# Float32r products whose moving operands are read in turn from two rows of a block

## The chip, the core and the metric

The kernel runs on one core of a Trainium2 chip. The metric is the time of one execution on the device in microseconds (us): 1568.5 us is the median of three runs of the kernel before the change (1567.9 to 1571.1). One further execution was profiled; its trace gives the start and the length of every instruction.

The engines have short names in the profile: PE is TensorE (its matmuls), PEld its weight loads, DVE is VectorE, ACT is ScalarE, POOL is GpSimd, SP is SyncE, which issues transfers here. A product `T.matmul(out, lhsT=..., rhs=...)` appears twice: as an LDWEIGHTS, which loads the stationary operand `lhsT` (128 rows by up to 128 columns), and as a MATMUL, which streams the moving operand `rhs` past it, column by column, and adds the result into a bank of PSUM.

## What is computed

Two layers of a decoder trunk on 512 positions of width 1024, in float32. Cut to what matters:

```python
for i in range(DEPTH):                                  # 2 layers
    z = rmsnorm(x, mix_pre_g[i]) @ w_in[i]              # 1024 -> 3206
    ...                                                 # gating, retention, forgetting attention on parts of z
    x = x + rmsnorm(concat([out_a, out_b, out_c]) @ w_o[i], mix_post_g[i])

    h = rmsnorm(x, ffn_pre_g[i])                        # 1024 -> 4096 -> 1024
    g, up = h @ w_gate[i], h @ w_up[i]
    x = x + rmsnorm((gelu(causal_conv3(g)) * up) @ w_down[i], ffn_post_g[i])

    gate = sigmoid(rmsnorm(x, ple_pre_g[i]) @ w_ple_gate[i])
    x = x + rmsnorm((p[i] @ w_ple_proj[i]) * gate, ple_post_g[i])
```

Nearly all the arithmetic is in the products with the weights.

## The kernel before, in words

**Products in three parts.** To keep float32 accuracy, a large product is made of three float32r products. `split` (ACT and DVE) writes an operand as a high and a low part, both float32r; `mm3` (line 908) issues high x high, high x low and low x high into the same bank. `down` (line 1277) writes the same three out by hand.

**Two kinds of product.** In the first, activations are stationary and weights move: 128 positions by up to 512 columns of weights (`tm_mm`, `tm_chunk_major`, `down`, `embed`). These make the gating and value projections, the output projection (`out_proj`), the down projection, the gate of the last sub-layer (`ple`) and the embedding product. Their moving operands are 512 columns wide, 384 and 390 for the two value projections, and 256 in the last chunk of the last layer. In the second kind, weights are stationary and activations move, so that the result comes out with features on the partitions: `fm_mm` (512 positions at a time) and `seven`.

**`seven` (line 860)** makes a pair of 128-feature blocks (gate and up, or two blocks of the mixers) for all 512 positions with seven products of half size in place of eight, by a scheme of sums and differences (Strassen's, in Winograd's form). Each of the seven products has four contraction blocks, three float32r products each, 256 positions wide. They go to three banks, `be`, `al` and `ga`; bank `be` accumulates over several of them and is copied out in between, so that the next product into `be` waits for the copy before it. ACT and DVE empty the banks into `gs` and `us` (256 columns at a time). It is called 78 times: 32 times per layer for gate and up, 7 times per layer in the mixers. The weights of a call come as one raw tile, whose sums are made by DVE and by adding transfers, and which are split before use (`seven_weights`, line 837).

**The feed-forward part.** `gate_up(b)` for 32 blocks `b` makes one call of `seven`, the convolution, gelu and product with `us`, and splits the result into `acts`. Between the sixth and the seventh product of the call, `pieces` puts the down products of four blocks earlier in, so that each block has 84 products of 256 columns and, from the fifth block on, 24 of 512.

**The order of the work** isn't the order of the program. All calls of engines are recorded by `Plan`; `Plan.issue` (line 252) simulates the five engines with a price for each instruction (`cost`, line 209), picks for each engine the next ready instruction, and then emits everything in the order so found. The price of a float32r product is 0.4427 ns per column. Dependencies come from the regions that instructions touch: `region` (line 149) turns an access pattern into runs of addresses. Large tiles lie in two pools, `X` and `W`, with a small pad between (line 60 and 540); the split weights of `seven` lie in `W`, all other float32r tiles in `X`, except `wu`, which lies in the small work pool.

**Weights in DRAM** are laid out by `packed` (line 503), in numpy on the host, before the launch.

Of the kernel before, what the change touches and what calls it, by code (L numbers as in the profile page):

```python
# [29 lines left out]
F32R = mybir.dt.float32r  # L30
# [3 lines left out]
ALU = mybir.AluOpType  # L34
AX = mybir.AxisListType

P = 128
# [13 lines left out]
class Plan:  # L51
# [96 lines left out]
    @staticmethod  # L148
    def region(ap):
        dims = [tuple(d) for d in ap.ap]  # L150
        step, parts = dims[0]
        p0, f0 = divmod(ap.offset, step) if step else (0, ap.offset)
        runs = [(f0, f0 + 1)]
        for st, n in reversed(dims[1:]):
            if st == 0 or n == 1:
                continue
            lo, hi = runs[0]
            if len(runs) == 1 and st <= hi - lo:
                runs = [(lo, hi + st * (n - 1))]
            else:  # L160
                runs = [(a + i * st, b + i * st) for i in range(n) for a, b in runs]
        return p0, p0 + parts, runs
# [46 lines left out]
    def cost(self, engine, method, outs, ins, args, kw):  # L209

        def size(ap):
            n = 1
            for d in ap.shape[1:]:
                n *= d
            return n

        if "dma" in method:
            return (820 if engine == "POOL" else 525) if outs[0].shape[0] > 2 else 700, 4.0 * size(outs[0]) * outs[0].shape[0]
        n = size(ins[0] if method == "tensor_reduce" else outs[0])
        psum = any(self.tiles[v.tensor.name][3] for v in ins + outs)  # L220
        scalars = [kw.get(k) for k in ("scalar", "scalar1", "scalar2", "bias", "scale")]
        pointers = sum(isinstance(v, bass.AP) for v in scalars)
        if engine == "PE":
            if method == "transpose":
                return 108, 0, n, "T"
            dt, rows = kw["lhsT"].dtype, kw["lhsT"].shape[0] / P
            if dt in (F32R, BF16):
                return (0.4427 if dt == F32R else 0.42) * n, 0, n * rows, n
            if kw["lhsT"].shape[0] == 64 or kw["lhsT"].shape[-1] == 64:
                return 0.5 * (n * 4 / 2.4 + 4), 0, 2 * n * rows, "H"  # L230
            return max(222, n * 4 / 2.4 + 4), 0, 2 * n * rows, "F"
        if engine == "ACT":
            func = ([v for v in args if isinstance(v, AF)] + [None])[0]
            self.table[len(self.ops)] = func if func in self.TABLES else None
            pointers += method == "mul" and isinstance(args[2], bass.AP)
            if outs[0].shape[0] < 64:
                return 160 + n / 1.196, 0
            return (50 if psum else 97) + n / 1.196 + 93 * pointers + 93 * ("accum_out" in kw), 0
        if engine == "POOL":
            if n > 64:  # L240
                return 155 + n * (2.09 if method == "tensor_tensor" else 0.86), 0
            if kw.get("op") == ALU.pow:
                return 600 + 155 * n, 0
            return 420, 0
        rate = 0.96
        if method == "reciprocal":
            rate /= 8
        elif method in ("tensor_copy", "tensor_scalar") and not psum:
            rate *= 2
        return 68 + 62 * bool(pointers) + 68 * ("accum_out" in kw) + n / rate, 0  # L250
# [249 lines left out]
SEVEN = ("hb11", "hb21", "hh6", "hhd", "hh7", "hb22", "hh4")  # L500


def packed(w):

    def rows(m, order=None):

        m = m.reshape(-1, P, m.shape[-1])
        return (m if order is None else m[list(order)]).transpose(1, 0, 2)

    def blocks(m):  # L510

        return m.reshape(KB, P, -1, P).transpose(2, 1, 0, 3).reshape(-1, P, KB * P)

    r = {}
    r["uv"] = [rows(m[:, C_U:C_U + 512]) for m in w["w_in"]]
    r["rv"] = [rows(m[:, C_RV:C_RV + 384]) for m in w["w_in"]]
    r["fv"] = [rows(m[:, C_FV:C_FV + 390]) for m in w["w_in"]]
    def pairs(g, u):
        g, u = (blocks(m).reshape(-1, P, 2, 512) for m in (g, u))
        return np.stack([u[:, :, 1], u[:, :, 0], g[:, :, 0], g[:, :, 1]], 2)  # L520

    r["rg"] = [blocks(m[:, C_RG + 2 * P:C_RG + 3 * P])[0] for m in w["w_in"]]
    r["fm"] = [pairs(*(np.concatenate([m[:, p[i]:p[i] + P] for p in PAIRS], 1) for i in range(2))) for m in w["w_in"]]
    r["gu"] = [pairs(g, u) for g, u in zip(w["w_gate"], w["w_up"])]
    r["dn"] = [m.reshape(8, 4, P, 2, 512).transpose(0, 3, 2, 1, 4) for m in w["w_down"]]
    r["wo"] = [np.stack([rows(m[:, c:c + 512], O_ORDER) for c in (0, 512)]) for m in w["w_o"]]
    r["pg"] = [np.stack([rows(m[:, c:c + 512]) for c in (0, 512)]) for m in w["w_ple_gate"]]
    r["pe"] = [rows(m) for m in w["w_ple_proj"]]
    return {k: np.ascontiguousarray(np.stack(v)) for k, v in r.items()}


def body(ctx, tc, a, out):
    nc = tc.nc
    plan = Plan(tc)
    V, A, G, T, SY = (plan.engine(n, e) for n, e in (
        ("DVE", nc.vector), ("ACT", nc.scalar), ("POOL", nc.gpsimd), ("PE", nc.tensor), ("SP", nc.sync)))
# [130 lines left out]
    class Plain:  # L667
# [21 lines left out]
        def rhs(self, i, k):  # L689
            return self.t[i][k // 4][:, k % 4, :]  # L690

        def lhs(self, i, k, c):
            return self.t[i][k // 4][:, k % 4, c * P:c * P + P]
# [166 lines left out]
    def seven(h, ws, gs, us, scale=1.0, between=None):  # L860

        wg, wu, sa, sb = ws
        be, al, ga = (bank(n)[:, 0:256] for n in ("beta", "alpha", "gamma"))
        t1, t2 = slice(0, 256), slice(256, 512)

        def product(ps, w, n, first, last, part=range(4)):
            for k in part:
                ks = slice(k * P, k * P + P)
                mm3(ps, lambda i: w[i][:, ks], lambda i: h.part(n, i, k), first and k == 0, last and k == 3, True)

        def part(t, i):
            return [t[:, j, i * 512:i * 512 + 512] for j in range(2)]
        product(be, part(wg, 0), "b11", True, False)
        A.copy(gs[:, t1], be)
        product(al, part(wg, 1), "b21", True, True)
        V.tensor_tensor(out=gs[:, t1], in0=al, in1=gs[:, t1], op=ALU.add)
        product(be, part(sa, 0), "h6", False, False)
        A.copy(gs[:, t2], be)
        product(ga, part(sa, 1), "hd", True, False)
        if scale == 1.0:  # L880
            A.copy(us[:, t2], ga)
        else:
            A.mul(us[:, t2], ga, -scale)
        product(be, part(sb, 0), "h7", False, False)
        V.scalar_tensor_tensor(out=us[:, t2], in0=be, scalar=-scale, in1=us[:, t2], op0=ALU.mult, op1=ALU.subtract if scale == 1.0 else ALU.add)
        product(ga, part(sb, 1), "b22", False, True)
        V.tensor_tensor(out=gs[:, t2], in0=ga, in1=gs[:, t2], op=ALU.add)
        rest = between() if between else None
        product(be, wu, "h4", False, True, range(1) if rest else range(4))
        if rest:  # L890
            rest()
            product(be, wu, "h4", False, True, range(1, 4))
        A.mul(us[:, t1], be, -scale)

    def tm_units(src, n, nk=KB, parts=2, more=None):

# [8 lines left out]
                ts.append(t)  # L905
        return lambda i, k, c0=0, c1=n: ts[k // 2][:, i, k % 2, c0:c1]

    def mm3(ps, lhs, rhs, first, last, skip=False):
        for i, (h, r) in enumerate(((0, 0), (0, 1), (1, 0))):
            T.matmul(ps, lhsT=lhs(h), rhs=rhs(r), start=first and i == 0, stop=last and i == 2, skip_group_check=skip)  # L910

    def tm_mm(ps, act, k, c, u, first, last, c0=0, c1=512, j=None):
        mm3(ps, lambda i: act.lhs(i, k, c), lambda i: u(i, k if j is None else j, c0, c1), first, last)
# [27 lines left out]
    def mixers(l, hT, uv, ready):  # L941
# [162 lines left out]
        def ret_gate():  # L1104
            ps = bank("gps")
            fm_mm(ps, hT, fm_units(a["w_rg"][l]))
            A.copy(sg[:, 2, :], ps)

        def ret_proj(p):
            res = [wk("rm") for _ in range(2)]  # L1110
# [139 lines left out]
    def ffn(l, hs, emb, ready, x, new, g, nxt):  # L1250
# [3 lines left out]
        ps = bank("cpps")  # L1254
# [22 lines left out]
        def down(q, c, u, done):  # L1277

            ps = bank("dn")
            ts = slice(c * P, c * P + P)  # L1280
            for j in range(4):
                t = acts[2 * q + j // 2]
                for i, (h, r) in enumerate(((0, 0), (0, 1), (1, 0))):
                    if j < 3 or not i:
                        T.matmul(ps, lhsT=t[:, h, j % 2, ts], rhs=u(r, j), start=j == 0 and i == 0, stop=False)

            def rest():
                T.matmul(ps, lhsT=t[:, 0, 1, ts], rhs=u(1, 3), start=False, stop=False)
                T.matmul(ps, lhsT=t[:, 1, 1, ts], rhs=u(0, 3), start=False, stop=True)
                done(ps)  # L1290
            return rest

# [241 lines left out]
```

## Time and profile before

| | |
|---|---|
| median of three runs | 1568.5 us (1567.9 to 1571.1) |
| span of the profiled execution | 1564.8 us |
| PE busy | 1546.8 us, 99% |
| DVE busy | 1219.5 us, 78% |
| ACT busy | 888.6 us, 57% |
| granted TensorE clock | 0.998 |
| HBM traffic | 152 GB/s over the span |

The span runs from the first to the last instruction of the program; the runs are timed around the whole execution, so a median is a few us longer than a span. The profile gives no other time for its own execution.

How to read it: matmuls are pipelined, and the profile models their ends, so that one MATMUL's duration (some 280 ns for 256 columns) is longer than its share of the time. The pace of products is read from the distance between starts: the start of a run of products to the start of what follows, divided by their count. A group "A<-B,C 128x256 f32 x936 | busy, mean" says what is written, what is read, the shape, the count, the time in which at least one of them was under way, and the mean duration of one in ns. Idle time stands behind the second bar, with who ended it. All instructions are emitted by one line of the planner, L452, so groups are told apart by the names of their tiles: `dn` is the bank of the down product, `beta`, `alpha` and `gamma` those of `seven`, `ps` those of the other weight-moving products, `wo` the first half of the output projection, `eps` the embedding, `gps` one gate block.

### The profile page before, as it was taken

The numbers are of one execution on the slowest core, as the hardware profiler recorded it, in microseconds if no ns is written. First come the engines' busy times: TensorE is split into PE (matmuls) and PEld (weight loads), VectorE is DVE, ScalarE is ACT, GpSimd is POOL, SyncE is SP. The second block draws the span as 40 slices with busy tenths as digits, with TensorE's granted clock in tenths as the row PEclk, the third lists the DMA queues.
The fourth block names the chain that finished last, engine by engine and source line by source line (L and its number), as shares of the span: only waits on it lengthen the run. The fifth ranks groups of instructions, "written<-read, shape, count | busy, mean of one in ns | idle before, by whom it ended". The sixth has DMA issues, their size and how long they took to land.

```text
span 1564.8 us, 26898 instructions
## 1 busy us (share of the span) xinstructions
PE 1546.8 (99%) x10554; PEld 1401.3 (90%) x10554; DVE 1219.5 (78%) x2036; ACT 888.6 (57%) x1501; POOL 193.3 (12%) x233
## 2 busy tenths in 40 slices
PE   9999999999999999999999999999999999999997
PEld 6998878999899999998889898799999999999986
DVE  6778978977778778767796789799677788687685
ACT  8556647765554545535584576586555455455362
POOL 1111112101101111000120101121101011011010
PEclk9999999999999999999999999999999999999999
DMA  9444529545637446456474346295546455455641
GB/s 331 92 123 104 180 90 291 134 121 142 169 81 198 137 96 176 130 156 247 155 216 102 85 122 210 76 301 136 145 112 155 143 136 147 128 150 148 232 158 54
DMA packets 87877, 239.00 MB, mean 153 GB/s; under 512 B 10036, under 2 KB 18364, under 8 KB 87752
## 3 DMA queue, kind: packets, MB, share of 16 engines
q1 hardware_dynamic: 64856, 195.81, 36.0%
q0 software_dynamic: 22464, 40.90, 16.4%
q8 instruction: 82, 1.34, 0.3%
q10 hardware_dynamic: 432, 0.59, 0.1%
q14 instruction: 43, 0.35, 0.1%
HBM read 219.94 MB, written 17.33 MB: 152 GB/s over the span
## 4 chain that ended last, share of the span: by engine, by line
PE 91%; ACT 3%; DMA 3%; DVE 2%; issue 1%; SPq 0%; POOLq 0%; POOL 0%; DVEq 0%; ACTq 0%
PE beta L452 26%; PE dn L452 21%; PE ps L452 14%; PE gamma L452 13%; PE alpha L452 6%; PE wo L452 3%; DMA graw<-in_w_gu_dram 2%; PE hps L452 1%; PE sps L452 1%; PE tps L452 1%; PE ops L452 1%; PE eps L452 1%; PE gps L452 1%; ACT thl L452 1%; PE rops L452 1%
## 5 line engine op out<-in xcount | busy, mean ns | idle before, releaser
L452 PE MATMUL dn<-thl,act 128*128 128x512 f32 x1536 | 370.5, 391 | 0.0
L452 PEld LDWEIGHTS dn<-thl,act 128*128 128x128 f32 x1536 | 280.4, 188 | 52.3
L452 PE MATMUL ps<-thl,hT 128*128 128x512 f32 (+3 forms) x984 | 209.7, 368 | 1.1 <-ACT hT L452 0.9
L452 POOL DMA_DIRECT2D graw<-in_w_gu_dram x128 | 112.4, 917 | 759.0 <-DVE wg L452 162.2
L452 PEld LDWEIGHTS ps<-thl,hT 128*128 128x128 f32 x984 | 175.1, 188 | 25.0 <-ACT hT L452 1.5
L452 DVE TENSOR_TENSOR thl<-traw,thl 128x1024 fp32r<-128x1024 f32 (+3 forms) x124 | 142.3, 1155 | 19.3 <-ACT thl L452 19.2
L452 ACT CAST thl<-traw 128x1024 fp32r<-128x1024 f32 (+3 forms) x124 | 121.3, 995 | 22.0 <-DVE wsb L452 8.9
L452 PEld LDWEIGHTS beta<-hh,wu 128*128 128x128 f32 x936 | 125.6, 188 | 9.1
L452 PE MATMUL beta<-hh,wu 128*128 128x256 f32 x936 | 130.2, 279 | 0.0
L452 PE MATMUL beta<-hh,wsa 128*128 128x256 f32 x936 | 122.0, 279 | 1.2 <-ACT gs L452 0.8
L452 PE MATMUL beta<-hh,wsb 128*128 128x256 f32 x936 | 120.5, 278 | 2.0 <-ACT gs L452 1.5
L452 PE MATMUL gamma<-hhd,wsa 128*128 128x256 f32 x936 | 121.7, 278 | 0.0
L452 DVE TENSOR_TENSOR wsb<-graw,wsb 128x1024 fp32r<-128x1024 f32 x78 | 95.3, 1222 | 29.5 <-PE beta L452 16.8
L452 PEld LDWEIGHTS beta<-hh,wsa 128*128 128x128 f32 x936 | 113.4, 188 | 2.6 <-ACT gs L452 1.4
L452 PEld LDWEIGHTS beta<-hh,wsb 128*128 128x128 f32 x936 | 112.9, 188 | 2.8 <-ACT gs L452 2.1
L452 DVE TENSOR_TENSOR graw<-graw 128x512 f32<-128x512 f32 x156 | 106.3, 686 | 10.8 <-DMA graw<-in_w_gu_dram 8.3
L452 PEld LDWEIGHTS gamma<-hhd,wsa 128*128 128x128 f32 x936 | 113.8, 188 | 0.0
L452 DVE TENSOR_TENSOR facc<-dn,facc 128x512 f32<-128x512 f32 x112 | 77.0, 687 | 45.1 <-PE dn L452 44.8
L452 DVE TENSOR_TENSOR wg<-graw,wg 128x1024 fp32r<-128x1024 f32 x78 | 95.2, 1220 | 15.8 <-ACT wg L452 8.7
L452 DVE TENSOR_TENSOR wsa<-graw,wsa 128x1024 fp32r<-128x1024 f32 x78 | 95.2, 1220 | 14.7 <-ACT wsa L452 14.6
L452 PE MATMUL beta<-hb,wg 128*128 128x256 f32 x768 | 100.5, 278 | 1.3 <-DVE hb L452 0.8
L452 DVE SCALAR_TENSOR_TENSOR cv<-gs,cw,cv 128x511 f32<-128x511 f32 (+1 forms) x128 | 95.3, 745 | 7.5 <-ACT cv L452 7.1
(225 smaller groups left out, 2625.4 us busy)
## 6 DMA issues: line engine op xcount, KB each, us to landing
graw<-in_w_gu_dram SPq DMA_DIRECT2D x128, 512.0 KB
graw<-in_w_gu_dram POOLq DMA_DIRECT2D x128, 256.0 KB, 5.4
traw<-in_w_dn_dram SPq DMA_DIRECT2D x64, 512.0 KB
x<-x SPq DMA_DIRECT2D x40, 512.0 KB
graw<-in_w_fm_dram SPq DMA_DIRECT2D x28, 512.0 KB
traw<-in_w_wo_dram SPq DMA_DIRECT2D x16, 512.0 KB
traw<-in_w_pg_dram SPq DMA_DIRECT2D x16, 512.0 KB
graw<-in_w_fm_dram POOLq DMA_DIRECT2D x28, 256.0 KB, 4.7
```

What stands on the lines that cost most here:

```text
L452: made = o[1](*[self.map(v) for v in o[2]], **{k: self.map(v) for k, v in o[3].items()})
```

## The change

A moving operand of n columns is seen as blocks of 256 columns (one block of n, if n isn't a multiple of 256), and each block as two rows of half its width. It is read in turn from the two rows: element 0 of the first row, element 0 of the second, element 1 of the first, and so on. `moving` makes that access pattern; a column's neighbour in reading order is then 128 elements, or 512 bytes, away (192 or 195 elements in the two value projections).

Results come out in reading order. Where weights move, `packed` lays their columns in DRAM so that reading order is the natural order (`turned`), and nothing else differs. Where activations move (`seven`, `fm_mm`), the columns of the bank are in reading order, and the instructions that empty it read every second column (`in_order`) and write in natural order (`halves`).

The planner's price for float32r and bfloat16 products becomes max(111.7, 2.6 + n / 2.4) ns, and `region` sorts the dimensions of an access pattern by step, so that the new pattern is taken as one run.

```diff
@@ Plan.region
-        for st, n in reversed(dims[1:]):
+        for st, n in sorted(dims[1:]):
@@ Plan.cost
             if dt in (F32R, BF16):
-                return (0.4427 if dt == F32R else 0.42) * n, 0, n * rows, n
+                return max(111.7, 2.6 + n / 2.4), 0, n * rows, n
@@ packed
+def block(n):
+    return 256 if n % 256 == 0 else n
+
 def packed(w):
 
+    def turned(m):
+        n = block(m.shape[-1])
+        m = m.reshape(*m.shape[:-1], -1, n // 2, 2)
+        return m.swapaxes(-1, -2).reshape(*m.shape[:-3], -1)
+
     def rows(m, order=None):
 
-        m = m.reshape(-1, P, m.shape[-1])
+        m = turned(m).reshape(-1, P, m.shape[-1])
...
-    r["dn"] = [m.reshape(8, 4, P, 2, 512).transpose(0, 3, 2, 1, 4) for m in w["w_down"]]
+    r["dn"] = [turned(m).reshape(8, 4, P, 2, 512).transpose(0, 3, 2, 1, 4) for m in w["w_down"]]
@@ seven
         product(be, part(wg, 0), "b11", True, False)
-        A.copy(gs[:, t1], be)
+        vbe, val, vga = (in_order(t) for t in (be, al, ga))
+        g1, g2, u1, u2 = (halves(t[:, ts]) for t in (gs, us) for ts in (t1, t2))
+        A.copy(g1, vbe)
         product(al, part(wg, 1), "b21", True, True)
-        V.tensor_tensor(out=gs[:, t1], in0=al, in1=gs[:, t1], op=ALU.add)
+        V.tensor_tensor(out=g1, in0=val, in1=g1, op=ALU.add)
...
-        A.mul(us[:, t1], be, -scale)
+        A.mul(u1, vbe, -scale)
@@ body
+    def moving(v):
+
+        n = block(v.shape[-1])
+        return v.rearrange("p (b s i) -> p b i s", s=2, i=n // 2)
+
+    def in_order(v):
+
+        return v.rearrange("p (b i s) -> p b s i", s=2, i=P)
+
+    def halves(v):
+
+        return v.rearrange("p (b s i) -> p b s i", s=2, i=P)
+
     def mm3(ps, lhs, rhs, first, last, skip=False):
         for i, (h, r) in enumerate(((0, 0), (0, 1), (1, 0))):
-            T.matmul(ps, lhsT=lhs(h), rhs=rhs(r), start=first and i == 0, stop=last and i == 2, skip_group_check=skip)
+            T.matmul(ps, lhsT=lhs(h), rhs=moving(rhs(r)), start=first and i == 0, stop=last and i == 2, skip_group_check=skip)
@@ ret_gate
-            A.copy(sg[:, 2, :], ps)
+            A.copy(halves(sg[:, 2, :]), in_order(ps))
@@ down
-                        T.matmul(ps, lhsT=t[:, h, j % 2, ts], rhs=u(r, j), start=j == 0 and i == 0, stop=False)
+                        T.matmul(ps, lhsT=t[:, h, j % 2, ts], rhs=moving(u(r, j)), start=j == 0 and i == 0, stop=False)
...
-                T.matmul(ps, lhsT=t[:, 1, 1, ts], rhs=u(0, 3), start=False, stop=True)
+                T.matmul(ps, lhsT=t[:, 1, 1, ts], rhs=moving(u(0, 3)), start=False, stop=True)
```

The other five instructions that empty the banks of `seven` are edited in the same way.

More of the change, by code (lines that the diff above doesn't have):

```diff
@@ L873, in seven @@
         product(be, part(wg, 0), "b11", True, False)
-        A.copy(gs[:, t1], be)
+        vbe, val, vga = (in_order(t) for t in (be, al, ga))
+        g1, g2, u1, u2 = (halves(t[:, ts]) for t in (gs, us) for ts in (t1, t2))
+        A.copy(g1, vbe)
         product(al, part(wg, 1), "b21", True, True)
-        V.tensor_tensor(out=gs[:, t1], in0=al, in1=gs[:, t1], op=ALU.add)
+        V.tensor_tensor(out=g1, in0=val, in1=g1, op=ALU.add)
         product(be, part(sa, 0), "h6", False, False)
-        A.copy(gs[:, t2], be)
+        A.copy(g2, vbe)
         product(ga, part(sa, 1), "hd", True, False)
         if scale == 1.0:
-            A.copy(us[:, t2], ga)
+            A.copy(u2, vga)
         else:
-            A.mul(us[:, t2], ga, -scale)
+            A.mul(u2, vga, -scale)
         product(be, part(sb, 0), "h7", False, False)
-        V.scalar_tensor_tensor(out=us[:, t2], in0=be, scalar=-scale, in1=us[:, t2], op0=ALU.mult, op1=ALU.subtract if scale == 1.0 else ALU.add)
+        V.scalar_tensor_tensor(out=u2, in0=vbe, scalar=-scale, in1=u2, op0=ALU.mult, op1=ALU.subtract if scale == 1.0 else ALU.add)
         product(ga, part(sb, 1), "b22", False, True)
-        V.tensor_tensor(out=gs[:, t2], in0=ga, in1=gs[:, t2], op=ALU.add)
+        V.tensor_tensor(out=g2, in0=vga, in1=g2, op=ALU.add)
         rest = between() if between else None
@@ L1284, in down @@
                     if j < 3 or not i:
-                        T.matmul(ps, lhsT=t[:, h, j % 2, ts], rhs=u(r, j), start=j == 0 and i == 0, stop=False)
+                        T.matmul(ps, lhsT=t[:, h, j % 2, ts], rhs=moving(u(r, j)), start=j == 0 and i == 0, stop=False)
             def rest():
-                T.matmul(ps, lhsT=t[:, 0, 1, ts], rhs=u(1, 3), start=False, stop=False)
-                T.matmul(ps, lhsT=t[:, 1, 1, ts], rhs=u(0, 3), start=False, stop=True)
+                T.matmul(ps, lhsT=t[:, 0, 1, ts], rhs=moving(u(1, 3)), start=False, stop=False)
+                T.matmul(ps, lhsT=t[:, 1, 1, ts], rhs=moving(u(0, 3)), start=False, stop=True)
                 done(ps)
```

## The prediction

> **What bounds the kernel now.** I read the page first, then the chain of waits, then what TensorE (PE) waited for, and last the timeline and the groups by shape, for the pace of single products.
>
> ```profile
> span 1564.8 us, 26898 instructions
> ...
> PE 1546.8 (99%) x10554; PEld 1401.3 (90%) x10554; DVE 1219.5 (78%) x2036; ACT 888.6 (57%) x1501; POOL 193.3 (12%) x233
> ...
> PE 91%; ACT 3%; DMA 3%; DVE 2%; issue 1%; SPq 0%; POOLq 0%; POOL 0%; DVEq 0%; ACTq 0%
> ```
>
> PE is busy for 1546.8 of 1564.8 us and is 91% of the chain that ended last. A busy PE could still be waiting inside, so the pace of its products has to be looked at. A piece of the chain in the second feed-forward part, and the longest run of one kind:
>
> ```profile
> 709.89 20.43 PE dn L452 x90
> ...
> 1104.12 5.01 PE dn L452 x22
> 1109.13 0.35 PE beta L452 x3
> 1109.48 0.47 PE dn L452 x2
> 1109.95 2.39 PE beta L452 x21
> 1112.34 1.36 PE alpha L452 x12
> ...
> 1119.14 5.01 PE dn L452 x22
> ```
>
> One feed-forward block takes 1119.14 - 1104.12 = 15.02 us, end to end on PE: 24 down products of 512 columns (5.48 us) and 84 gate/up products of 256 columns (9.54 us). A 512-column product takes 20.43 / 90 = 227.0 ns, a 256-column one 1.36 / 12 = 113.3 ns. PE waits for nobody there:
>
> ```profile
> PE beta L452 <- ACT gs L452: 2.4, 5, 0.6
> ```
>
> is its longest wait on an engine in the whole run. So the time of this kernel is the number of products times their pace, and what the change can do, it does to the pace.
>
> **Where the pace comes from.** Four more rows: the bfloat16 products of the start, once the clock is full; a run of 256-column products at the end of the last layer; a run of 390-column products.
>
> ```profile
> 6.91 0.81 PE L452 MATMUL idle<-idle 128*128 128x512 bf16 x3
> 7.55 0.60 PE L452 MATMUL pps<-k_ident,pr 128*128 128x128 f32 x4
> ```
>
> ```profile
> L452 PE MATMUL ps<-thl,hT 128*128 128x256 f32 x46 | 5.7, 283 | 0.0
> ```
>
> ```profile
> L452 PE MATMUL ps<-thl,hT 128*128 128x390 f32 x83 | 14.9, 339 | 0.0
> ```
>
> Three bfloat16 products of 512 columns take 7.55 - 6.91 = 0.64 us, 213 to 216 ns each; I use 215.5. If such a product streams one column per cycle and little else, the clock is about 2.4 GHz (512 / 215.5 = 2.38, an estimate), and one column per cycle is 213.3 ns for 512, 162.5 for 390 and 106.7 for 256 columns. The float32r products take 227.0; (14.9 - 0.34) / 82 = 177.6; and (5.7 - 0.28) / 45 = 120.4. So they lie 13.7, 15.1 and 13.7 ns above it: about the same for each product, whatever its columns. The loss isn't a slower rate per column; it comes once per product, that is, once per weight load. And it depends on where the operands lie: in the gate/up products (weights in another pool than the moving operand) it is 113.3 - 106.7 = 6.6 ns, but in some of the mixers' products of the same shape
>
> ```profile
> 73.09 1.58 PE L452 MATMUL alpha<-hT,wg 128*128 128x256 f32 x12
> 74.51 1.58 PE L452 MATMUL beta<-hh,wsa 128*128 128x256 f32 x12
> ```
>
> it is 1.42 us / 12 = 118.3 - 106.7 = 11.6 ns. A loss per weight load that depends on the places of the two operands reads as a collision of the weight load's reads with the moving reads. The order of the moving reads is a lever on such a collision; that is the argument for the change, and it is an inference, since no row shows a moving operand read in another order. The Trainium skill ("TensorE: Matmul & The Clock Gate", on LDWEIGHTS in the step-by-step part) says the opposite: the two reads have ports of their own and the next load takes nothing from the running product. The rows above disagree with that, by 13.7 ns per product; by the page the change could do nothing here (the first rival).
>
> **A floor.** Products shorter than their weight load show its pace:
>
> ```profile
> 168.39 0.55 PE L452 MATMUL rops<-mix,inn 128*128 128x64 f32 x4
> 168.77 0.44 PE L452 MATMUL rops<-R,qd 128*128 128x128 f32 x2
> 169.05 0.56 PE L452 MATMUL rops<-mix,inn 128*128 128x64 f32 x4
> ...
> 170.39 0.33 PE L452 MATMUL rops<-mix,inn 128*128 128x64 f32 x2
> ```
>
> 18 instructions from 168.39 to 170.39 are 111.1 ns each, though they stream 64 or 128 columns. A 256-column product can't go below about 111.3, even without any collision.
>
> **The change, part by part.** Counts:
>
> ```profile
> L452 PE MATMUL dn<-thl,act 128*128 128x512 f32 x1536 | 370.5, 391 | 0.0
> L452 PE MATMUL ps<-thl,hT 128*128 128x512 f32 x552 | 131.8, 394 | 1.1 <-ACT hT L452 0.9
> L452 PE MATMUL beta<-hh,wu 128*128 128x256 f32 x936 | 130.2, 279 | 0.0
> ...
> L452 PE MATMUL wo<-thl,cc 128*128 128x512 f32 x192 | 51.1, 406 | 0.0
> L452 PE MATMUL ps<-thl,cc 128*128 128x512 f32 x192 | 46.3, 395 | 0.0
> L452 PE MATMUL ps<-thl,hT 128*128 128x384 f32 x192 | 38.0, 345 | 0.0
> L452 PE MATMUL ps<-thl,hT 128*128 128x390 f32 x192 | 34.5, 339 | 0.0
> ...
> L452 PE MATMUL eps<-ehl,pT 128*128 128x512 f32 x96 | 23.8, 399 | 0.5 <-ACT pT L452 0.2 <-DVE ehl L452 0.2
> ...
> L452 PE MATMUL gps<-hT,fhl 128*128 128x512 f32 x48 | 13.2, 411 | 0.0
> ```
>
> The 512-column products are 1536 + 552 + 192 + 192 + 96 + 48 = 2616. `seven` has seven equal products, so 7 x 936 = 6552 of 256 columns.
>
> 1. *Moving reads in turn from two rows* (`moving`). If the collision goes, a 512-column product falls from 226.7 to 215.5 (the bfloat16 row): 2616 x 11.2 = 29.3 us. The 390-column ones fall by about 13 (177.6 to 164.7) and the 384-column ones, whose run isn't clean enough for a pace, by the same 11.2: 192 x 24 = 4.6 us. The 48 of the last chunk: 120.4 to 111.3, 0.4 us. The 6552 go from 113.3 to the floor; between the floor's row and 111.7, which the changed planner writes, 1.6 to 2.2 ns, 10.5 to 14.4 us; I take 12. Mixers' pairs are 14 of the 78; if all of them were at 118.3, they bring another 14 x 84 x 5 = 5.9 us; I take half, 3. Sum 49.3 us.
> 2. *Emptying the banks in order* (`in_order`). The same count of instructions and elements, but ScalarE (ACT) and VectorE (DVE) now read every second element of a bank. No row shows an inner step of two. It can't be cheaper; the dear end is half rate:
>
> ```profile
> L452 ACT CAST wu<-graw 128x512 fp32r<-128x512 f32 x78 | 48.2, 619 | 1.5 <-DMA graw<-in_w_gu_dram 1.1
> L452 ACT COPY gs<-beta 128x256 f32<-128x256 f32 x128 | 47.3, 370 | 28.6 <-PE beta L452 28.0
> ```
>
> ```profile
> L452 DVE TENSOR_TENSOR wu<-graw,wu 128x512 fp32r<-128x512 f32 x78 | 53.0, 686 | 7.1 <-ACT wu L452 6.1
> ...
> L452 DVE TENSOR_TENSOR gs<-alpha,gs 128x256 f32<-128x256 f32 x64 | 26.9, 421 | 6.6 <-PE alpha L452 6.6
> ```
>
> ```profile
> 318.00:678.00 360.00, 358.69 (x2581) 335.13 (x2580) 275.06 (x378) 191.39 (x294) 41.18 (x47) 1.00 0.52 138
> ```
>
> 256 more elements are 249 ns on ACT and 265 on DVE; with four and three such readings per block, at most 1.0 and 0.8 us more. In the feed-forward stretch DVE is busy 275.06 of 360 us and ACT 191.39, 11.5 and 8.0 us of each 15.0, so neither becomes the bound even at 14.5 us per block. What could reach PE is the bank `be`: its next product waits for the copy to `gs`, with one 1.36 us product as cover for a 0.37 us copy. That wait is 2.4 us in all now, and the change adds no other; at half rate it is perhaps 6 more (behind the late copy stand ACT's casts of the next weights, which have slack of several us at 53% busy). I take 2, near the cheap end, because the element count is the same.
> 3. *Weights turned in DRAM* (`packed`): done on the host; every array keeps its shape, so the transfers keep their number, size and queue. Nothing.
> 4. *The planner's prices and `region`*: the order of work is written from the new prices, so neighbours may swap and PE may meet other short waits. All its idle time now is 1564.8 - 1546.8 = 18 us; I bound this by 5 us either way and take 0.
>
> Sum: 1564.8 - 49.3 + 2 = 1517.5 us of span. The runs' median, 1568.5, is 3.7 us above the profiled span, so 1521. A feed-forward block should come to 24 x 215.5 + 84 x 111.4 = 14.53 us. Least gain in this case: 29.3 + 4.6 + 0.4 with nothing on the 256-column products, less 6 and 5: 23 us, 1545. Most: 29.3 + 4.6 + 0.4 + 14.4 + 5.9 + 5, 60 us, 1508.
>
> **The rivals.** *Nothing happens*: the loss belongs to the weight load itself and not to the order of the moving reads; products stay at 227.0 and 113.3, and the time at 1566 to 1572. For it speaks that it is a fixed cost per load; against it, that it halves with another placing of the operands.
>
> *Slower, because each read falls on a new line.* Read in order, neighbouring columns lie side by side; read in turn, each is 512 bytes from the last. If the reader fetches a stretch and can't hold two, every column costs a second cycle. Products at two cycles per column exist here:
>
> ```profile
> 142.52 1.89 PE L452 MATMUL sps<-mix,mix 128*128 128x256 f32 x8
> ```
>
> (1.89 - 0.28) / 7, about 216 to 230 ns for 256 columns. Then 2616 x 202 + 6600 x 103 + 384 x 150 = 528 + 680 + 58, 1266 us more: 2835. It decides as soon as a column costs more than 17/16 cycle (227.0 / 213.3). Against it: in contiguous reading the loss doesn't grow with the columns, so crossing from stretch to stretch is free there; that says little about one column per stretch. The Trainium skill ("SBUF — State Buffer", the note on cachelines under Door 1) states this rule: lines of 16 bytes, at least two hits on each needed for full bandwidth, four fp32 as the reach of a free stride. By it the change would be this rival. No run here shows it.
>
> *The banks take it back*: if the stepped readings make PE wait 0.25 us at each of the two `be` copies of the 78 calls, 156 x 0.25 = 39 us of the gain go: about 1559. Against it: the cover of 1.36 us, and five waits in all now.
>
> **How the numbers follow.** The forecast has 0.82: the rows speak for a collision, and a collision depends on the order. Nothing 0.05, new lines 0.09, banks 0.04. The range 1508 to 1545 is the forecast's own and holds 8 in 10. A measurement of this kernel can tell about 0.2%, 3 us, from no change. Faster: 0.82 + 0.04 = 0.86; same 0.05; slower 0.09.
>
> **What would show it.** Right: runs of dn at 215 to 216 ns, twelve 256-column products in 1.34 us, the block at 14.5 us, one pace for all placings, ACT copies of `gs` near 370 ns, PE still at 99%. Wrong: dn at 227 (nothing), above 230 (new lines), or idle time of PE behind ACT `gs` (banks).

## The result, and the profile after

The changed kernel takes 1528.4 us (median of four runs, 1527.4 to 1530.1) against 1568.2 us before: a ratio of 0.9748, 95% interval 0.9734 to 0.9761. The profiled execution has a span of 1526.9 us and took 1528.6 us in all.

The page of the changed kernel:

```profile
span 1526.9 us, 26942 instructions
...
PE 1496.3 (98%) x10554; PEld 1383.6 (91%) x10554; DVE 1216.7 (80%) x2036; ACT 888.9 (58%) x1501; POOL 194.3 (13%) x233
...
PE 74%; DVE 8%; DMA 5%; ACT 5%; issue 5%; POOL 1%; SPq 0%; POOLq 0%; DVEq 0%; ACTq 0%
```

PE's busy time fell by 1546.8 - 1496.3 = 50.5 us, the span by only 37.9. The rest is idle time of PE: 1526.9 - 1496.3 = 30.6 us, where it was 18.0. The chain says the same in other words: PE fell from 91% to 74% of it.

One feed-forward block of the second layer, in the chain, and the longest run of down products:

```profile
1048.99 4.75 PE dn L452 x22
...
1056.86 1.34 PE alpha L452 x12
...
1063.56 0.65 PE dn L452 x3
...
1445.41 19.00 PE dn L452 x88
```

The block now takes 1063.56 - 1048.99 = 14.57 us in place of 15.02. A 512-column product takes 19.00 / 88 = 215.9 ns (227.0 before), a 256-column one 1.34 / 12 = 111.7 (113.3). Three more groups of the changed kernel: the mixers' products (timeline), the 256-column products of the last chunk, and a run of 390-column products (groups by shape):

```profile
74.08 1.50 PE L452 MATMUL gamma<-hhd,wsa 128*128 128x256 f32 x12
75.42 1.50 PE L452 MATMUL beta<-hh,wsb 128*128 128x256 f32 x12
```

```profile
L452 PE MATMUL ps<-thl,hT 128*128 128x256 f32 x48 | 5.5, 275 | 0.0
```

```profile
L452 PE MATMUL ps<-thl,hT 128*128 128x390 f32 x91 | 15.4, 331 | 0.0
```

Twelve mixers' products take 1.34 us, 111.7 ns each, where some took 118.3. The last chunk is at (5.5 - 0.28) / 47 = 111 (120.4 before), the 390-column run at (15.4 - 0.33) / 90 = 167.4 (177.6 before). One pace for all placings, then: of the 6552 products of `seven`, 6428 now stand 105 to 112 ns apart, where 4656 stood 113 to 114 and 1771 stood 117 to 119.

The copies out of the banks, ACT and DVE, now reading every second element:

```profile
L452 ACT COPY gs<-beta 128x256 f32<-128x256 f32 x128 | 47.9, 374 | 25.5 <-PE beta L452 25.2
```

374 ns, and 419 for the DVE addition into `gs`; before, 370 and 421. A step of two costs next to nothing there. The longest waits of PE after the change:

```profile
PE beta L452 <- ACT gs L452: 3.2, 5, 1.4
PE tps L452 <- DVE fet L452: 2.9, 2, 1.5
PE beta L452 <- DVE wsa L452: 2.6, 2, 2.2
PE hps L452 <- DVE h L452: 2.5, 5, 0.6
```

The new idle time isn't one wait. It is fifteen of 0.5 to 2.2 us, where there were six, mostly in the mixers and where one stage passes into the next; inside the feed-forward part PE is still busy for nearly all of the time:

```profile
300.00:700.00 400.00, 398.58 (x2946) 380.48 (x2945) 309.41 (x427) 215.41 (x330) 41.94 (x48) 1.00 0.55 149
```

To see which products gave what, I summed, from the two traces, the distances from each product's start to the next instruction's start on PE, without idle time:

| product | count | before, us | after, us | difference |
|---|---|---|---|---|
| 512 columns | 2616 | 608.0 | 576.2 | -31.8 |
| 384 and 390 columns | 384 | 70.2 | 65.8 | -4.4 |
| last chunk, 256 columns | 48 | 5.6 | 5.2 | -0.4 |
| `seven`, 256 columns | 6552 | 758.3 | 744.1 | -14.2 |

That makes 50.8 us; the busy time says 50.5.

### The profile page after: what moved, and what is told of

Read it like the earlier page. It is cut to its first block, busy times and chain, and to the rows that moved or that the text cites. A ratio compares the mean times of both kernels' runs of the same rounds, so it can differ in the third digit from the quotient of the medians.

```text
span 1526.9 us, 26942 instructions
## 1 busy us (share of the span) xinstructions
PE 1496.3 (98%) x10554; PEld 1383.6 (91%) x10554; DVE 1216.7 (80%) x2036; ACT 888.9 (58%) x1501; POOL 194.3 (13%) x233
## 4 chain that ended last, share of the span: by engine, by line
PE 74%; DVE 8%; DMA 5%; ACT 5%; issue 5%; POOL 1%; SPq 0%; POOLq 0%; DVEq 0%; ACTq 0%
PE beta L452 20%; PE dn L452 19%; PE ps L452 13%; PE gamma L452 11%; PE alpha L452 5%; DMA graw<-in_w_gu_dram 3%; DMA traw<-in_w_dn_dram 2%; PE wo L452 1%; ACT rr L452 1%; PE hps L452 1%; DVE cv L452 1%; PE tps L452 1%; PE ops L452 1%; ACT junk L452 1%; POOL y L452 1%
## 5 line engine op out<-in xcount | busy, mean ns | idle before, releaser
L452 PE MATMUL dn<-thl,act 128*128 128x512 f32 x1536 | 351.7, 380 | 0.0
L452 PE MATMUL ps<-thl,hT 128*128 128x512 f32 (+3 forms) x984 | 198.7, 358 | 2.5 <-ACT hT L452 2.4
L452 PEld LDWEIGHTS ps<-thl,hT 128*128 128x128 f32 x984 | 171.6, 189 | 19.5 <-ACT hT L452 2.9
L452 PE MATMUL beta<-hh,wu 128*128 128x256 f32 x936 | 126.2, 275 | 1.0 <-DVE us L452 0.9
L452 ACT CAST wsa<-graw 128x1024 fp32r<-128x1024 f32 x78 | 82.0, 1051 | 43.2 <-PE gamma L452 24.7
L452 ACT CAST wg<-graw 128x1024 fp32r<-128x1024 f32 x78 | 82.1, 1053 | 30.5 <-PE gamma L452 13.2
```

The costliest lines, as they stand in the source:

```text
L452: made = o[1](*[self.map(v) for v in o[2]], **{k: self.map(v) for k, v in o[3].items()})
```

## The experiments

Two questions were open: where the 12.6 us of new idle time come from, and why the order of reading changes the pace at all.

**The order of work or the pace?** The new prices also write a new order, so the two have to be taken apart. The first kernel is the changed one with the old price; all engines' instructions then stand in the order of before.

```diff
-                return max(111.7, 2.6 + n / 2.4), 0, n * rows, n
+                return (0.4427 if dt == F32R else 0.42) * n, 0, n * rows, n
```

> The new reading with the old prices of the planner, so that all engines' work stands in the order of before. After the change the products are 50.5 us shorter in all and PE is idle 12.6 us more (30.6 of 1526.9 us against 18.0 of 1564.8). Theory 'order': the new idle time comes from the order that the new prices make. Then the paces are those after the change, 216 and 111.7 ns, PE's idle time falls back to about 18 us, and the time is about 1516 us. Theory 'speed': a faster PE leaves the other engines less time ahead of it, whatever the order. Then the idle time stays at 30 us or grows, since this order was reckoned for a slower PE: 1528 us or more.

Measured: 1525.6 us, ratio 0.9730 (0.9716 to 0.9745).

```profile
PE 1495.9 (98%) x10554; PEld 1380.6 (91%) x10554; DVE 1216.2 (80%) x2036; ACT 885.5 (58%) x1501; POOL 193.1 (13%) x233
```

PE is busy as long as after the change, and of the span of 1523.6 us idle for 27.7: 9.7 more than the same order had with the slower products. Two waits make 5.0 of it; before, then with the old prices:

```profile
PE beta L452 <- ACT gs L452: 2.4, 5, 0.6
PE hps L452 <- DVE h L452: 1.3, 3, 0.5
```

```profile
PE beta L452 <- ACT gs L452: 4.6, 7, 1.4
PE hps L452 <- DVE h L452: 4.1, 10, 0.7
```

Next, the kernel before with the new price alone, that is, the old reading in the order of after:

```diff
-                return (0.4427 if dt == F32R else 0.42) * n, 0, n * rows, n
+                return max(111.7, 2.6 + n / 2.4), 0, n * rows, n
```

> The reading of before with the new prices, so that the work stands in the order of after. Order: paces 227 and 113.3 ns as before, idle time of PE near 30 us: about 1580 us. Speed: a slow PE hides the other engines in this order too: idle near 18 us, 1568 us.

Measured: 1571.5 us (ten runs), ratio 1.0026 (1.0014 to 1.0037).

```profile
PE 1544.3 (99%) x10554; PEld 1399.2 (89%) x10554; DVE 1221.0 (78%) x2036; ACT 890.6 (57%) x1501; POOL 194.5 (12%) x233
```

Of 1566.9 us idle for 22.6, 4.6 more than before (by the medians of that comparison, 1571.5 against 1567.4, it is 4.1). The longest single wait of the changed kernel is there too, at the old pace, and not in the old order at either pace, so it belongs to the new order:

```profile
PE beta L452 <- DVE wsa L452: 2.2, 1, 2.2
```

So both theories hold a part: the faster products (with the stepped copies, 374 ns for 370) add 8 to 10 us of idle time in either order (18.0 to 27.7, 22.6 to 30.6), the new order alone 3 to 5 us at either pace (18.0 to 22.6, 27.7 to 30.6). Each of these is one profiled execution.

The changed kernel, unedited, and the kernel with the old prices were timed once more side by side, with a third that tries to win the idle time back.

> The kernel after the change once more, beside the next two on one chip: ratio 0.975.

> The new reading with the planner's old prices once more, beside the kernel after. Order: 2 to 4 us below it, ratio 0.9725 to 0.9735. If the order doesn't matter: the same as it.

Measured: 1527.6 us (ratio 0.9749, 0.9736 to 0.9762) for the kernel after, 1525.0 us (0.9727, 0.9714 to 0.9741) with the old prices. The four runs of the one (1527.3 to 1529.7) lie above the four of the other (1523.5 to 1525.4), as in the comparisons above: the changed reading with the old prices is the fastest version found, by about 2.7 us. Their profiles give 26.1 us of idle time with the old prices and 30.5 after the change.

The third reckons more for the engines that come late:

```diff
                     busy, nbytes = ops[i][6][:2]
+                    busy *= 1.05 if e in ("ACT", "DVE") else 1
```

> The kernel after the change, where the planner reckons 5% more for each instruction of ACT and DVE and so puts their work earlier against PE's. The two prices runs gave 18 us of idle time with the old order made fast, and 23 with the new. If the idle time is neighbours that come late because PE is faster, and planning them longer brings them forward: idle time of 15 us or less, about 1520 us. If it is the engines' own load and latency: no change, 1526 to 1530 us.

Measured: 1530.2 us, ratio 0.9767 (0.9754 to 0.9780), and 1528.2 - 1496.6 = 31.6 us idle. It wins nothing; the expectation of 1520 was wrong. (It also has a figure wrong: the old order made fast had 27.7 us of idle time; 18 is the old order at the old pace.) Whether any order would get back to the 18 us of before isn't settled by three orders.

**Each half of the change alone.** Both kernels have the order of work of the changed kernel, instruction for instruction. In the first, `seven` and the gate block read plainly and empty their banks plainly (the emptying is shown; their products lose `moving`, and the gate block's copy its `halves` and `in_order`):

```diff
-        vbe, val, vga = (in_order(t) for t in (be, al, ga))
-        g1, g2, u1, u2 = (halves(t[:, ts]) for t in (gs, us) for ts in (t1, t2))
+        vbe, val, vga = be, al, ga
+        g1, g2, u1, u2 = (t[:, ts] for t in (gs, us) for ts in (t1, t2))
```

> Only the products with moving weights read in turn; the calls of seven and the gate block read plainly and empty their banks plainly. Order of work as after. Products of 512, 384 and 390 columns at 216, 163 and 167 ns, those of seven at 113.3 to 118: by the prediction's terms 29.3 - 0.5 + 4.6 + 0.4 = 34 us less than before, 1534 us, plus up to 12.6 us of idle time if that comes from the order (1547).

Measured: 1551.4 us, ratio 0.9891 (0.9874 to 0.9908): 16 us gained on the 1567.4 of that comparison, less than expected even with the idle time. In the second, the other way round, only `seven` and the gate block read in turn (shown for the weights in DRAM and the down product; the other products with moving weights lose `moving` too):

```diff
-        m = turned(m).reshape(-1, P, m.shape[-1])
+        m = m.reshape(-1, P, m.shape[-1])
...
-                        T.matmul(ps, lhsT=t[:, h, j % 2, ts], rhs=moving(u(r, j)), start=j == 0 and i == 0, stop=False)
+                        T.matmul(ps, lhsT=t[:, h, j % 2, ts], rhs=(u(r, j)), start=j == 0 and i == 0, stop=False)
```

> Only the calls of seven and the gate block read in turn; products with moving weights, and the weights in DRAM, as before. Order of work as after. Products of seven at 111.7, of 512 columns at 227 ns: by the prediction's terms 15 to 16 us less than before, 1552 us, plus up to 12.6 us of idle time if that comes from the order (1565).

Measured: 1558.8 us, ratio 0.9945 (0.9929 to 0.9962): 8.6 us gained. The halves give 24.6 us, the whole 39.8. Two things make the difference. The idle time comes with each half: PE is idle for 30.2 us in the one and 26.5 us in the other, 12.2 and 8.5 more than before, and only once in the whole. And in the first half alone the plain products of `seven` became slower than they had been: their sum, made as in the table above, is 767.8 us, where the kernel before has 758.3. The chain of that kernel in the feed-forward part:

```profile
368.06 1.41 PE alpha L452 x12
369.48 1.39 PE beta L452 x12
370.87 1.36 PE gamma L452 x12
...
382.96 1.41 PE alpha L452 x12
384.37 1.41 PE beta L452 x12
385.79 1.41 PE gamma L452 x12
```

Products of one shape go at (385.79 - 382.96) / 24 = 117.9 ns through a whole block and change to 113.3 in the middle of another. Three instants out of many, but they agree with the count: about 2900 of 6552 distances lie at 117 to 119 there, some 1800 in the kernel before, and some 900 in the kernel with the new prices alone, which has the same order of work and so the same tiles in the same places. So plain reading has two paces, a stretch of products stays in one, and the place of the operands alone doesn't decide which.

**What the reader doesn't like.** Two kernels put runs of 36 products ahead of the changed kernel, each run with another moving pattern or another stationary operand, on tiles of ones (`mv` moving, `st` stationary, and the tile `wg` in the other pool as a second stationary one). Nobody reads these results, and the time of the whole isn't compared; each was executed once. The core of it, shortened:

```python
def pace(name, rhs, lhsT, count=36):
    ps = bank(name)
    for i in range(count):
        T.matmul(ps[0:lhsT.shape[-1], 0:n], lhsT=lhsT, rhs=rhs, start=True, stop=True)   # n: columns of rhs

def turns(v, dist, rows=2):
    return v.rearrange("p (b s i) -> p b i s", s=rows, i=dist)

pace("plain", mv[:, 0:512], st[:, 0:128])
pace("colsa", mv[:, 0:512], st[:, 0:64])
pace("turntg", turns(mv[:, 0:512], 4), st[:, 0:128])
...
```

> The kernel after the change, with runs of 36 float32r products each put in at its start, on tiles of ones, whose results nobody reads (so its time is longer by these runs and isn't compared). Each run has another moving pattern or stationary operand. Theory 'collision': the loss comes from the weight load's reads. Then plain 512-column products go at 226.7 ns with 128 stationary columns, at about 220 with 64 and 217 with 32; 128- and 256-column products are bound by their load, near 111 plus at most 13; the place of the stationary operand matters. Theory 'start': a float32r product pays 13 ns to start, whatever its load: 226.7 with 64 and 32 stationary columns too. On the patterns: if what counts is that the reader leaves a stretch of neighbours at each column, then two rows 4, 8, ... 256 elements apart, four rows, and a plain step of 4 all go at 215.8, and a step of 2 or rows 2 apart don't; if it is a matter of the distance between rows (banks), then only some distances do. Rows of pairs, fours and eights in turn show how short the stretches have to be. If each fresh stretch cost a second cycle, turns would go at 427.

From the timeline of the first (start, time under way, then what; the pace is the distance from one start to the next, divided by 36):

```profile
24.04 8.45 PE L452 MATMUL colsa<-bmv,bst 128*64 128x512 f32 x36
32.33 8.50 PE L452 MATMUL colsb<-bmv,bst 128*32 128x512 f32 x36
40.67 8.56 PE L452 MATMUL byfour<-bmv,bst 128*128 128x512 f32 x36
...
133.26 7.93 PE L452 MATMUL turntg<-bmv,bst 128*128 128x512 f32 x36
141.03 8.32 PE L452 MATMUL turnth<-bmv,bst 128*128 128x512 f32 x36
149.19 7.93 PE L452 MATMUL turncols<-bmv,bst 128*64 128x512 f32 x36
...
172.50 10.35 PE L452 MATMUL rowsfour<-bmv,bst 128*128 128x512 f32 x36
182.69 12.41 PE L452 MATMUL pairs<-bmv,bst 128*128 128x512 f32 x36
194.93 9.18 PE L452 MATMUL fours<-bmv,bst 128*128 128x512 f32 x36
...
212.70 16.47 PE L452 MATMUL steptwo<-bmv,bst 128*128 128x512 f32 x36
228.99 16.79 PE L452 MATMUL stepfour<-bmv,bst 128*128 128x512 f32 x36
245.60 4.20 PE L452 MATMUL shortturn<-bmv,bst 128*128 128x256 f32 x36
...
249.77 4.36 PE L452 MATMUL shortw<-bmv,wg 128*128 128x256 f32 x36
...
266.90 4.40 PE L452 MATMUL shortwagain<-bmv,wg 128*128 128x256 f32 x36
```

With 64 stationary columns a plain product takes (32.33 - 24.04) / 36 = 230.3 ns, with 32 it takes 231.7: no less than with 128, where the runs settle at 226.7 or, as `byfour` (49.07 - 40.67) / 36, at 233.3. At 512 columns the loss doesn't grow with the load; "collision" is out in that form. "Start", the same loss for each product, fits these rows but not the 256-column ones, which lose 6.6 ns at 113.3. Two rows in turn, 256, 128, 64, 32, 16, 8 and 4 (`turntg`) elements apart, all go at 215.8 (217.2 at 256, where a single product took 269); 2 apart (`turnth`), inside the same 16 bytes, at 226.7, as plainly. Four rows in turn (`rowsfour`) take 283, two rows by pairs 340, by fours 250 and by eights 243, and a plain step of 2 or 4 takes 452 and 461. So it isn't enough to leave the 16 bytes at each column; of the patterns of this kernel, only two rows with one column each are faster than plain reading. The last two lines shown have the same tiles and the same shape: 30 of the 36 products of `shortw` stand 113 or 114 ns apart, all 36 of `shortwagain` 117 to 119. With the stationary operand in `st` three such runs settled at 120, so that the place has some part in it isn't excluded.

> As the run before it: runs of 36 products on tiles of ones at the start of the kernel after the change, results unread. It showed 230 to 232 ns with 64 and 32 stationary columns, so the loss doesn't shrink with the load's columns, and a step of 2 or 4 at 453 to 461. Theory 'load', in what is left of it: any load, even of 2 columns, disturbs the moving reads once; with 2 columns the loss is 5 ns or less. Theory 'stretch': the reader of the moving operand loses by itself on four neighbours (16 bytes) read one after the other, and the load only shifts where; then 2 stationary columns still give 226 to 234 ns at 512 columns, and 113 to 120 at 256. Then one column read 512 times, or each column twice, should change the loss, and bfloat16 at a step of 2 (four columns per 16 bytes) should lose as float32r does, while plain bfloat16 is at 216. Rows 6, 5 and 3 elements apart in turn: at 216 if only leaving the 16 bytes counts, between 216 and 227 where rows share them.

```profile
48.27 8.51 PE L452 MATMUL colstwo<-bmv,bst 128*2 128x512 f32 x36
56.61 6.43 PE L452 MATMUL longall<-bmv,bst 128*128 128x384 f32 x36
...
81.66 4.46 PE L452 MATMUL shortall<-bmv,bst 128*128 128x256 f32 x36
85.95 4.25 PE L452 MATMUL shortsixtyfour<-bmv,bst 128*64 128x256 f32 x36
...
94.12 4.24 PE L452 MATMUL shorttwo<-bmv,bst 128*2 128x256 f32 x36
98.20 8.67 PE L452 MATMUL fromone<-bmv,bst 128*128 128x512 f32 x36
...
115.13 7.94 PE L452 MATMUL bfplain<-bbf 128*128 128x512 bf16 x36
122.91 8.29 PE L452 MATMUL bfbytwo<-bbf 128*128 128x512 bf16 x36
131.04 16.42 PE L452 MATMUL bfbyfour<-bbf 128*128 128x512 bf16 x36
147.28 32.58 PE L452 MATMUL bfbyeight<-bbf 128*128 128x512 bf16 x36
179.68 17.62 PE L452 MATMUL bfturn<-bbf 128*128 128x512 bf16 x36
...
204.79 8.81 PE L452 MATMUL turnfive<-bmv,bst 128*128 128x510 f32 x36
213.44 9.84 PE L452 MATMUL turnthree<-bmv,bst 128*128 128x510 f32 x36
...
255.01 4.09 PE L452 MATMUL turnshortcols<-bmv,bst 128*64 128x256 f32 x36
258.94 4.09 PE L452 MATMUL turnshorttwo<-bmv,bst 128*2 128x256 f32 x36
```

With a load of two columns a plain 512-column product still takes (56.61 - 48.27) / 36 = 231.7 ns, a 256-column one 113.3: these losses are there with next to no load. One part does hang on the load: at 256 columns `shortall`, with 128 stationary columns, takes (85.95 - 81.66) / 36 = 119.2, and with 64, 32 or 2 it is 113 to 114. "Stretch" holds for reading in sequence: bfloat16, plain at 216.1, loses as soon as it has four columns per 16 bytes (step 2: 225.8), and step 4 and 8 give 451 and 900. All of these are one number: 225.8 / 128, 451 / 256 and 900 / 512 are 1.76 ns per 16 bytes, as are float32r plainly (226.7 / 128 = 1.77) and at a step of 2 (452 / 256 = 1.77). Four columns at full pace need 4 x 0.42 = 1.68 ns (215.8 / 512 = 0.42). So, as the simplest reading of these rows, the reader in sequence brings 16 bytes per 1.77 ns, 5% too slow for four-byte columns and fast enough for two-byte ones; on top come a few ns per product that settle in one pattern or another. Two more runs fit: one column read 512 times goes at 219 ns and each column read twice at 216, and both bring fewer bytes. And the limit isn't the array's: the granted clock is 1.00 from 147.3 to 152 us of this kernel and 0.50 from 152.1 to 179.6, both within `bfbyeight`, whose products stand 899 to 900 ns apart throughout. `bfturn` begins at half the clock and ends at the full one, and but for the first its products stand 483 to 486 ns apart.

Some of it doesn't fit. Float32r at a step of 4 takes 461 / 512 = 0.90 ns per 16 bytes. Two rows 6 elements apart go at 212.5 ns for 504 columns, as they should, but 5 apart at 240 and 3 apart at 269 for 510, though 5 elements are more than 16 bytes: both outside the expected 216 to 227. And no run shows why two rows in turn escape the limit while pairs and four rows fare worse. The floor of 111.7 goes with the weight load: in turn, a 256-column product takes 111.7 with 128 stationary columns and (258.94 - 255.01) / 36 = 109.2 with 64, and no less with 2.

## Why the prediction was right, and where it wasn't

The time fell into the range, 7 us above the forecast of 1521, and by the effect that was forecast: the products' pace. The reason given for that effect, a collision with the weight load, was wrong (3), so it was luck in part that this way of reading helps: four rows in turn, which take the reader from its neighbours just as well, would have cost 283 ns in place of 227.

1. *PE's pace is the bound*: right. PE's busy time fell by 50.5 us and the span by 37.9 of that; PE is busy for 98% of it still.
2. *The new paces*: right. Forecast 215.5 and 111.3 ns and a block of 14.53 us; measured 215.9, 111.7 and 14.57. By kind, 29.3 us against 31.8 (512 columns), 4.6 against 4.4, 0.4 against 0.4, and 15 against 14.2 for `seven`. The first is more because the 512-column products stood 608.0 / 2616 = 232.4 ns apart on the mean before, not 226.7. The 390-column products came to 167.4, not 164.7.
3. *Where the loss comes from*: wrong, though the sum went by other rows and didn't suffer. The text took 13.7, 15.1 and 13.7 ns for one loss per weight load, a collision of the load's reads with the moving ones. The load has no part in the loss at 512 columns (231.7 ns with two stationary ones). The loss is 0.09 ns per 16 bytes, so it does grow with the columns, as the two commonest rows, 113.3 and 227.0, said by being 1 to 2; the rows at 118, 120 and 177.6 carried the extra few ns of a pattern that had settled, and I read them as the rule. At 256 columns that extra showed only with 128 stationary columns (119.2 against 113.3), so there the load does count. The "place of the operands" was mostly such a pattern too: it changed in the midst of a stage, with the tiles where they were. The rows shown for it could not carry it: the mixers' `beta<-hh,wsa` at 118.3 has its weights in the same pool as in the feed-forward part, where 545 of 576 such products before the change (300 to 700 and 1090 to 1430 us) stood less than 116 ns apart.
4. The Trainium skill ("TensorE: Matmul & The Clock Gate", LDWEIGHTS in the step-by-step part), which lets the next load take nothing from the running product, was held to disagree with the trace. The 512-column rows don't disagree with it: their loss is the same with two stationary columns. Whether the 119.2 and 113.3 ns of the 256-column ones do, no run shows, since a load of 128 columns is itself near its floor there (111.7 against 109.2). What the prediction concluded from the page, that the change could do nothing, is refuted.
5. *New lines* (slower): refuted for two rows in turn, but not a phantom: a plain step of 2 costs 452 ns, and bfloat16 read in turn about 484. The Trainium skill ("SBUF — State Buffer", the note on cachelines under Door 1) names the 16 bytes that also show here: 2 apart and 4 apart differ just there, and the bfloat16 rows come to one time per 16 bytes. That two hits per line suffice for full bandwidth doesn't hold for this reader: float32r at a step of 2 has two hits and half the pace.
6. *Emptying the banks*: the term was 2 us; the copies take 374 ns in place of 370, and PE's wait for `gs` is 3.2 us in place of 2.4 (4.6 in the old order). The rival of the banks, 39 us, is out.
7. *The order and the idle time*: the mis-sized term. The text gave 0 to it and bounded it by 5 us; PE's idle time grew by 12.6 us. It reckoned with swapped neighbours (3 to 5 us, which the bound held) and left out that a PE faster by 3% finds the other engines as slow as before: 8 to 10 us in an unchanged order. That these engines had been only just ahead is my reading of the waits for `gs` and `h` above.

The sum closes: 1517.5 us of span forecast, plus 12.6 - 2 of idle time, less 50.5 - 49.3 of pace, is 1526.9, the span measured. The profiled execution lies 1.7 us above it, not 3.7.

## What to carry to other kernels

When all products of a shape run at an odd pace, vary one thing at a time in runs of a few dozen products: pattern, width, stationary columns, type. Two such kernels told more of the cause than the rows of the full trace. Where float32r operands move, two rows read in turn, one column each, took 0.42 ns per column at every even distance tried from 4 to 256 elements; check that nothing else (2, 3 or 5 elements apart, pairs, four rows, steps, bfloat16) is taken for the same. And when the bound engine gets faster by a few per cent, budget the idle time it will meet: here 12.6 of the 50.5 us, a quarter, of which 3 to 5 came with the new order.

## What the runs showed of the hardware that I hadn't expected

- The moving reader brings 16 bytes of a partition per 1.76 to 1.77 ns in sequence, whether float32r or bfloat16; four-byte columns need 1.68.
- That time doesn't follow the granted clock of PE: bfloat16 at a step of 8 takes 900 ns per product at 1.00 and at 0.50.
- Two rows in turn: 215.8 ns for 512 float32r columns, 226.7 plainly, and about 484 for bfloat16, which takes 216.1 plainly.
- Plain products of 256 columns have two paces, 113.3 and 117.8, and keep one for whole blocks; above 113 to 114 they went only with 128 stationary columns.
- ACT and DVE read every second element of a bank as fast as neighbours (374 and 419 ns for 256, where 370 and 421 were).
